# A two-layer decoder trunk: the first norm from raw rows with its vector per partition, and the group norm's turns moved to the chain's end and into the second projection

## The chip, the cores and the metric

The kernel runs on one core of a Trainium2 chip. Its time is the device time of one execution, in microseconds (us); the profile shows one execution engine by engine. TensorE (PE) multiplies matrices and transposes, VectorE (DVE), ScalarE (ACT) and GpSimd (POOL) work element by element, and transfers are issued from queues of SyncE (SP), ScalarE and POOL. TensorE's clock has two levels, 2.4 and 1.2 GHz; the profile shows what was granted, as a share of the higher.

## The reference

The input x is 256 tokens of 1024 values; there are two layers, and everything is float32. What is computed, cut down:

```python
for layer in range(2):
    h = rms_norm(x, ffn1_norm[layer])                    # x * rsqrt(mean(x*x) + eps) * g
    x = x + 0.5 * swiglu_ffn(h, ffn1_w_gu[layer], ffn1_w_down[layer])
    h = rms_norm(x, mix_norm[layer])
    p = h @ w_in                                         # gates a and b, u, v, and r, k, v, decay for the time mixing
    y_a = chunked_sgu(u_a, v_a, ...)
    y_b, v_first = rwkv7_time_mix(p_b, v_first, ...)     # a state of 64x64 per head, 16 heads, token by token
    merged = sigmoid(gate_a) * (y_a @ w_proj_a[layer]) + sigmoid(gate_b) * (y_b @ w_proj_b[layer])
    x = x + merged @ w_out[layer]
    h = rms_norm(x, ffn2_norm[layer])
    x = x + 0.5 * swiglu_ffn(h, ffn2_w_gu[layer], ffn2_w_down[layer])
return rms_norm(x, final_norm)
```

At the end of the time mixing each head of 64 values is normalised (the group norm), multiplied by gn_g, shifted by gn_b, and a bonus is added:

```python
y = (y - mu) * lax.rsqrt(var + GN_EPS)
y = y.reshape(bsz, t, B_WIDTH) * gn_g + gn_b
y = y + bonus.reshape(bsz, t, B_WIDTH)
```

## The kernel before

The 256 tokens are two blocks of 128 (tb 0 and 1). A matrix product is done in three matmuls per tile of 128 rows (`mm3`, L236 to L238): both factors are split in a high part and a low rest, and high by high, high by low and low by high are added in PSUM. "A matmul" without more means one of these, 128x512; 48 of them make a chunk: 512 columns, both blocks, 8 row tiles.

All weights come through one stream. `plan` writes down their order in units of 512 KB; `pump` issues their loads on SP's queue into three raw buffers (`wr`), and `emit_split` cuts each into `wh` (a cast on ScalarE, L220) and `wl` (a subtract on VectorE, L221), four units ahead of use. So the two engines have a weight split each 2.7 us, and whatever else they do stands between splits.

Activations are wanted with the row dimension on partitions. `transpose_split` transposes four tiles of 128x128 on TensorE (L318), casts the high part out of PSUM on ScalarE (L322), and takes the low rest on VectorE (L323).

The start: x's two blocks (512 KB each) and the first norm's vector, copied to all partitions (512 KB, L328), are loaded; VectorE multiplies x by the vector (L344), TensorE transposes, ScalarE and VectorE split, and the first chunk begins. The norm's factor per token (`rf`, L349, L350) is applied later, at the gates. `chunk_a` with token_first uses four units for block 0 and then the same four for block 1, so that block 1 may come later.

The time mixing ends in `rwkv_chain`: four steps c of 64 tokens. In each, small matmuls (64x64) make the state's input (`given` L884, L895), solve (L905), update the state (L924, with VectorE's L929 and L930), and after every second step give the output y of one token block (L942, L950). Each block's y is copied to SBUF, squared and scaled on VectorE by `rwkv_scale` (L971, L974, with a power on POOL, L973), for two groups g of four tiles. `rwkv_turn` then loads the bonus (L984), transposes (L988), multiplies and shifts with one activation per tile (L992), adds the bonus (L994) and splits (L996, L997) into `ybT`, the input of the second projection (w_proj_b). `weave` puts the chain's steps between units of other products (`gated`: gates and the first projection), so TensorE has work while a step waits for the other engines. When the chain ends, the rest of these products is done, `before()` issues the loads of the next norm on POOL's queue, and the second projection runs.

A scheduler with priorities makes each engine's order from this at build time. At run time every engine follows its own order strictly, and waits where an instruction's input isn't there.

## Time and profile before

| | |
|---|---|
| time, median of 3 runs | 1450.06 us (1449.78 to 1453.37) |
| time of the profiled execution | 1450.86 us |
| its span | 1449.2 us |
| TensorE busy | 1377.2 us (95%) |
| VectorE busy | 894.7 us (62%) |
| ScalarE busy | 735.6 us (51%) |
| mean granted clock | 0.986 |

The span is the time from the profiled execution's first to its last instruction. An engine's busy time leaves out the time in which it waits. The timeline gives for each instruction, or for a run of equal ones, its start, its length and, in brackets, how long the engine stood idle before it and what released it.

### The profile page before, as it was taken

How to read it: one execution, taken by the hardware profiler on the slowest of the kernel's cores; microseconds unless marked ns; L12 is line 12 of the kernel's file. 1: busy time of each engine (PE TensorE's matmuls, PEld its weight loads, DVE VectorE, ACT ScalarE, POOL GpSimd, SP SyncE). 2: the span in 40 equal slices, each digit the busy share in tenths (PEclk: the TensorE clock that was granted, in tenths of full speed). 3: DMA queues.
4: the chain of work that ended last, by engine and by line, in shares of the span. 5: the costliest groups of instructions: out<-in, count | busy, mean ns of one | idle time of the engine just before them, and what ended most of it. 6: DMA issues, size and time to landing. Idle time of an engine off the chain costs nothing. (4 is left out here: it accounts for less than half of the span.)

```text
span 1449.2 us, 21790 instructions
## 1 busy us (share of the span) xinstructions
PE 1377.2 (95%) x8642; PEld 1155.3 (80%) x8642; DVE 894.7 (62%) x1216; ACT 735.6 (51%) x1033; POOL 138.2 (10%) x200
## 2 busy tenths in 40 slices
PE   6999999999899999999999999999988989999996
PEld 5888879887787778888888888898867767788885
DVE  4555466769874565555555554769788636555553
ACT  5444456646555545444454443765655545545442
POOL 5000011113102110000010000110140011100000
PEclk9999999999989999999999999999999899999999
DMA  7755557443443567665576655674434425665552
GB/s 230 236 185 190 179 174 239 145 140 117 148 144 88 189 212 230 188 188 181 185 260 188 189 180 187 198 224 134 145 117 145 132 74 189 225 208 180 189 187 88
DMA packets 116871, 254.64 MB, mean 176 GB/s; under 512 B 8878, under 2 KB 12096, under 8 KB 116768
## 3 DMA queue, kind: packets, MB, share of 16 engines
q1 hardware_dynamic: 108048, 226.00, 48.7%
q0 software_dynamic: 8576, 26.72, 5.5%
q8 instruction: 68, 1.11, 0.3%
q10 hardware_dynamic: 144, 0.52, 0.1%
q14 instruction: 35, 0.29, 0.1%
HBM read 243.77 MB, written 9.44 MB: 175 GB/s over the span
## 5 line engine op out<-in xcount | busy, mean ns | idle before, releaser
L221 DVE TENSOR_TENSOR wl<-wr,wh 128x1024 fp32r<-128x1024 f32 x427 | 523.0, 1227 | 392.2 <-ACT wh L220 388.2
L220 ACT CAST wh<-wr 128x1024 fp32r<-128x1024 f32 x427 | 448.5, 1052 | 507.6 <-PE g L238 388.9
L236 PE MATMUL g<-wh,z 128*128 128x512 f32 x1088 | 431.5, 397 | 2.4 <-ACT z L322 2.4
L238 PE MATMUL g<-wh,z 128*128 128x512 f32 x1088 | 430.4, 396 | 3.3 <-DVE z L323 3.3
L237 PE MATMUL g<-wl,z 128*128 128x512 f32 x1088 | 429.2, 394 | 0.5 <-DVE wl L221 0.5
L238 PEld LDWEIGHTS g<-wh,z 128*128 128x128 f32 x1088 | 205.7, 189 | 48.5 <-DVE z L323 6.4
L236 PEld LDWEIGHTS g<-wh,z 128*128 128x128 f32 x1088 | 206.1, 189 | 45.2 <-ACT z L322 4.1
L237 PEld LDWEIGHTS g<-wl,z 128*128 128x128 f32 x1088 | 206.0, 189 | 43.2 <-DVE wl L221 1.7
L236 PE MATMUL g<-wh,w 128*128 128x512 f32 x416 | 162.9, 392 | 0.0
L237 PE MATMUL g<-wl,w 128*128 128x512 f32 x416 | 162.2, 390 | 0.0
L238 PE MATMUL g<-wh,w 128*128 128x512 f32 x384 | 149.7, 390 | 0.0
L296 PE MATMUL g<-z,wh 128*128 128x256 f32 x384 | 109.5, 285 | 0.0
L297 PE MATMUL g<-z,wl 128*128 128x256 f32 x384 | 109.3, 285 | 0.0
L294 PE MATMUL g<-z,wh 128*128 128x256 f32 x384 | 108.9, 284 | 0.0
L237 PEld LDWEIGHTS g<-wl,w 128*128 128x128 f32 x416 | 78.1, 188 | 15.8
L236 PEld LDWEIGHTS g<-wh,w 128*128 128x128 f32 x416 | 78.1, 188 | 15.7
L238 PEld LDWEIGHTS g<-wh,w 128*128 128x128 f32 x384 | 72.1, 188 | 14.9
L297 PEld LDWEIGHTS g<-z,wl 128*128 128x128 f32 x384 | 73.6, 192 | 0.5 <-issue 0.5
L296 PEld LDWEIGHTS g<-z,wh 128*128 128x128 f32 x384 | 73.7, 192 | 0.2 <-issue 0.2
L294 PEld LDWEIGHTS g<-z,wh 128*128 128x128 f32 x384 | 73.6, 192 | 0.2 <-issue 0.2
L318 PE MATMUL m<-ident,z 128*128 128x128 f32 x336 | 50.8, 277 | 17.0 <-DVE z L344 8.4
L472 POOL DMA_DIRECT2D xspill<-w x10 | 5.7, 574 | 601.7 <-DVE w L456 601.7
(232 smaller groups left out, 1256.0 us busy)
## 6 DMA issues: line engine op xcount, KB each, us to landing
wr<-in_ffn_w_gu_dram SPq DMA_DIRECT2D x176, 512.0 KB, 3.6
wr<-in_ffn_w_down_dram SPq DMA_DIRECT2D x88, 512.0 KB, 3.5
wr<-in_w_in_rest_dram SPq DMA_DIRECT2D x58, 512.0 KB, 3.5
wr<-in_w_in_first_dram SPq DMA_DIRECT2D x57, 512.0 KB, 4.0
wr<-in_w_proj_a_dram SPq DMA_DIRECT2D x16, 512.0 KB, 3.7
wr<-in_w_proj_b_dram SPq DMA_DIRECT2D x16, 512.0 KB, 3.7
wr<-in_w_out_dram SPq DMA_DIRECT2D x16, 512.0 KB, 4.0
xspill<-w POOLq DMA_DIRECT2D x10, 512.0 KB, 3.3
```

Source lines behind the costliest of these rows:

```text
L220: nc.scalar.copy(hi, raw)
L221: nc.vector.tensor_tensor(lo, raw, hi.bitcast(F32), ALU.subtract)
L236: mm(ps, lhsT=xh, rhs=wh, start=first, stop=False)
L237: mm(ps, lhsT=xh, rhs=wl, start=False, stop=False)
L238: self.last_mm = mm(ps, lhsT=xl, rhs=wh, start=False, stop=last).ins
L294: mm(o, lhsT=hi[:, k, cs], rhs=xh[kt // 4][:, kt % 4, :], start=(kt == 0 and b % 2 == 0), stop=False, skip_group_check=True)
L296: mm(o, lhsT=hi[:, k, cs], rhs=xl[kt // 4][:, kt % 4, :], start=False, stop=False, skip_group_check=True)
L297: mm(o, lhsT=lo[:, k, cs], rhs=xh[kt // 4][:, kt % 4, :], start=False, stop=kt == NK - 1, skip_group_check=True)
L318: nc.tensor.transpose(ps[:, i * P:(i + 1) * P], src[:, i * P:(i + 1) * P], self.ident)
L472: self.nc.gpsimd.dma_start(self.xsrc[tb], self.x[tb])
```

## The change

The first norm. Its vector is loaded as 8 rows of 128 values (4 KB), transposed and copied once, so that it stands per partition (`gain`). x is loaded in halves of 256 KB on SP's and ScalarE's queues, the second block behind two weight loads and two casts. TensorE transposes x itself; the vector is multiplied in when the result leaves PSUM, 128 columns at a time (ScalarE L138, VectorE L140 of the new text). The second block's turn, the squares and the factor per token of both blocks follow the first unit's six matmuls of the first chunk.

The group norm's turns. Those of token block 0, until now between the third and the fourth step of the chain (c == 2), come at the chain's end. Those of block 1, until now two steps of other work behind the chain, come into the second projection's first chunk, behind 18 matmuls (three units of block 0). In the new text the group norm's lines are L1027 (reduce), L1028 and L1029 (POOL), L1030 (scale), L1044 (transposes), L1048 (activations), L1050 (add), L1052 and L1053 (split); the chain's are L942 (`given`), L953, L963 (solve), L979 (state's input), L984 and L985 (state), L997 and L1005 (output). A weight split is L272 and L273.

```diff
+    def first_norm(self, vec, xt):
+        nc = self.nc
+        rows = self.cp.tile([NK, P], F32, name="grows")
+        nc.sync.dma_start(rows, vec.rearrange("(k p) -> k p", p=P))
+        self.x = [self.wt([P, D]) for _ in range(NTB)]
+        def load(tb):
+            r = []
+            for j, q in enumerate((nc.sync, nc.scalar)):
+                js = slice(512 * j, 512 * j + 512)
+                r.append(q.dma_start(self.x[tb][:, js], self.xsrc[tb][:, js]))
+            return r[0].ins
+        def turn(tb):
+            for j in range(2):
+                ps = self.mp().rearrange("p (k t) -> p k t", t=P)
+                for k in range(4):
+                    nc.tensor.transpose(ps[:, k, :], self.x[tb][:, (4 * j + k) * P:(4 * j + k + 1) * P], self.ident)
+                part = lambda p, k: xt[p][j][:, k, tb * P:tb * P + P]
+                g = lambda k: gain[:, 4 * j + k:4 * j + k + 1]
+                for k in range(4):
+                    hi = nc.scalar.activation(part(0, k), ps[:, k, :], AF.Identity, scale=g(k))
+                for k in range(4):
+                    lo = nc.vector.scalar_tensor_tensor(part(1, k), ps[:, k, :], g(k), part(0, k).bitcast(F32),
+                                                        ALU.mult, ALU.subtract)
+            return hi.ins, lo.ins
+        behind = self.tc.issue_after
+        first = load(0)
+        self.first_consts()
+        ps = self.mp()[:, 0:NK]
+        nc.tensor.transpose(ps, rows, self.ident[0:NK, 0:NK])
+        gain = self.cp.tile([P, NK], F32, name="gain0")
+        nc.vector.tensor_copy(gain, ps)
+        hi, lo = turn(0)
+        with behind(first), behind(hi), behind(lo):
+            self.pump(2)
+            load(1)
+        self.norm_begin()
+        def rest():
+            hi, lo = turn(1)
+            with behind(hi):
+                for tb in range(NTB):
+                    for j in range(2):
+                        self.square(tb, j)
+                    self.rf[tb] = self.norm_factor(tb, "rf")
+        return rest
 
...
-    def pump(self):
+    def pump(self, limit=1 << 30):
...
-            while self.n_load < min(len(self.units), self.n_used + RAW_BUFS + HL_BUFS - 1):
+            while self.n_load < min(limit, len(self.units), self.n_used + RAW_BUFS + HL_BUFS - 1):
...
                 us.append(self.take())
                 go(0, us[i], 2 * i)
+                if between and between[0] == i:
+                    with self.tc.issue_after(self.last_mm):
+                        between[1]()
...
+    def square(self, tb, j):
+        self.nc.scalar.activation(self.tt([P, 512]), self.x[tb][:, 512 * j:512 * j + 512], AF.Square, scale=1.0 / 32,
+                                  accum_out=self.ss[tb][:, j:j + 1])
...
-        rf = self.rf
...
-            ps = self.chunk_a(ht, ci == 0)
+            ps = self.chunk_a(ht, ci == 0, None if ci else between)
...
-                    nc.scalar.activation(t[:, tb, :g1 - c0], ps[tb][:, :g1 - c0], AF.Silu, scale=rf[tb])
+                    nc.scalar.activation(t[:, tb, :g1 - c0], ps[tb][:, :g1 - c0], AF.Silu, scale=self.rf[tb])
...
-    def load_x(self, queues):
+    def load_x(self):
         self.x = [self.wt([P, D]) for _ in range(NTB)]
         for tb in range(NTB):
-            queues[tb].dma_start(self.x[tb], self.xsrc[tb])
+            self.nc.gpsimd.dma_start(self.x[tb], self.xsrc[tb])
...
             yield
-            if c == 2:
-                for g in range(2):
-                    turn(g, 0, ys[g])
             if c < 3:
                 ps_next, last = given(c + 1)
...
-        yield
-        yield
+            if c == 1:
+                early = ys
         for g in range(2):
-            turn(g, 1, ys[g])
+            turn(g, 0, early[g])
...
-            ps = self.chunk_a(ybT, j == 0)
+            ps = self.chunk_a(ybT, j == 0, None if j else (2, self.late))
...
         with self.tc.high_priority(offset=8000):
-            before(a["ffn1_norm"][0])(True)
-            self.first_consts()
-            self.norm_begin()
-            for tb in range(NTB):
-                for j in range(2):
-                    self.norm_half(tb, j, self.g)
-                after(tb)
+            state["ht"] = self.ht()
+            rest = self.first_norm(a["ffn1_norm"][0], state["ht"])
...
-            self.ffn(l, "ffn1", state["ht"], before(a["mix_norm"][l], True), after, None if l else tables)
+            self.ffn(l, "ffn1", state["ht"], before(a["mix_norm"][l], True), after, None if l else tables,
+                     None if l else (0, rest))
```

ScalarE's order at the program's start, before. Here w is x, z the norm's result, m PSUM of transposes, wh a weight's high part:

```order
L464 DMA w_87<-in_x_dram 128x1024
L343 ACT_TABLE_LOAD
L343 ACTIVATE t_102,ss_99<-w_86 128x512
L343 ACTIVATE t_105,ss_99<-w_86 128x512
L343 ACTIVATE t_130,ss_100<-w_87 128x512
L343 ACTIVATE t_133,ss_100<-w_87 128x512
L220 CAST wh_155<-wr_153 128x1024
L220 CAST wh_161<-wr_159 128x1024
L322 CAST z_108<-m_115 128x4x128
L220 CAST wh_167<-wr_165 128x1024
L322 CAST z_109<-m_122 128x4x128
L220 CAST wh_173<-wr_171 128x1024
L322 CAST z_108<-m_139 128x4x128
L322 CAST z_109<-m_146 128x4x128
```

ScalarE's order at the same place after the change:

```order
L127 DMA w_92<-in_x_dram 128x512
L138 ACT_TABLE_LOAD
L138 ACTIVATE z_86<-m_107,gain_105 128x128 x4
L138 ACTIVATE z_87<-m_120,gain_105 128x128 x4
L272 CAST wh_135<-wr_133 128x1024
L272 CAST wh_141<-wr_139 128x1024
L127 DMA w_93<-in_x_dram 128x512
L272 CAST wh_151<-wr_149 128x1024
L138 ACTIVATE z_86<-m_179,gain_105 128x128 x4
L272 CAST wh_157<-wr_155 128x1024
L138 ACTIVATE z_87<-m_192,gain_105 128x128 x4
```

The four squares at the head are gone from here. Eight scaled copies stand ahead of the first cast instead of the squares, and the load of the second block's second half stands behind two casts.

VectorE's order in layer 0 from the first scale of block 0 (L971), before. Here gv is the scale's factor, t the output y and its square, w and ld the two halves of `ybT`:

```order
L971 TENSOR_REDUCE gv_4073<-t_4071 128x8
L974 TENSOR_TENSOR t_4068<-t_4068,gv_4073 128x512
L971 TENSOR_REDUCE gv_4083<-t_4081 128x8
L221 TENSOR_TENSOR wl_4445<-wr_4316,wh_4444 128x1024
L974 TENSOR_TENSOR t_4078<-t_4078,gv_4083 128x512
L994 TENSOR_TENSOR t_4071<-t_4071,t_4165 128x512
L997 TENSOR_TENSOR w_3714<-t_4071,w_3712 128x4x128
L929 TENSOR_TENSOR state_4220<-m_4211,state_3985 128x256
L994 TENSOR_TENSOR t_4081<-t_4081,t_4179 128x512
L930 TENSOR_TENSOR state_4220<-state_4220,ec_1821 128x256
```

VectorE's order in layer 0 from the same scale (now L1027), after:

```order
L1027 TENSOR_REDUCE gv_4097<-t_4095 128x8
L1030 TENSOR_TENSOR t_4092<-t_4092,gv_4097 128x512
L1027 TENSOR_REDUCE gv_4107<-t_4105 128x8
L1030 TENSOR_TENSOR t_4102<-t_4102,gv_4107 128x512
L273 TENSOR_TENSOR wl_4469<-wr_4312,wh_4468 128x1024
L984 TENSOR_TENSOR state_4216<-m_4207,state_4009 128x256
L985 TENSOR_TENSOR state_4216<-state_4216,ec_1845 128x256
L984 TENSOR_TENSOR state_4228<-m_4219,state_4021 128x256
L985 TENSOR_TENSOR state_4228<-state_4228,ec_1845 128x256
L1027 TENSOR_REDUCE gv_4401<-t_4399 128x8
```

The turn's add and subtract (L994, L997) are gone from here, and the four updates of the state, which were mixed with them, stand together behind both scales and a weight subtract. On TensorE 74 matmuls of other products stand between the turns of block 0, at the chain's end, and the second projection.

VectorE's order in layer 1 from the first scale of block 1, before:

```order
L971 TENSOR_REDUCE gv_10698<-t_10696 128x8
L974 TENSOR_TENSOR t_10693<-t_10693,gv_10698 128x512
L221 TENSOR_TENSOR wl_10879<-wr_10840,wh_10878 128x1024
L971 TENSOR_REDUCE gv_10708<-t_10706 128x8
L974 TENSOR_TENSOR t_10703<-t_10703,gv_10708 128x512
L221 TENSOR_TENSOR wl_10897<-wr_10858,wh_10896 128x1024
L994 TENSOR_TENSOR t_10696<-t_10696,t_10753 128x512
L997 TENSOR_TENSOR w_10007<-t_10696,w_10005 128x4x128
L994 TENSOR_TENSOR t_10706<-t_10706,t_10767 128x512
L1037 SCALAR_TENSOR_TENSOR z_10835<-z_10835,g_10921 128x512
```

VectorE's order in layer 1 from the same scale, after:

```order
L1027 TENSOR_REDUCE gv_10694<-t_10692 128x8
L1030 TENSOR_TENSOR t_10689<-t_10689,gv_10694 128x512
L273 TENSOR_TENSOR wl_10857<-wr_10813,wh_10856 128x1024
L1027 TENSOR_REDUCE gv_10704<-t_10702 128x8
L1030 TENSOR_TENSOR t_10699<-t_10699,gv_10704 128x512
L273 TENSOR_TENSOR wl_10875<-wr_10836,wh_10874 128x1024
L1050 TENSOR_TENSOR t_10388<-t_10388,t_10709 128x512
L1050 TENSOR_TENSOR t_10398<-t_10398,t_10723 128x512
L273 TENSOR_TENSOR wl_10893<-wr_10854,wh_10892 128x1024
L1053 TENSOR_TENSOR w_10031<-t_10388,w_10029 128x4x128
L1053 TENSOR_TENSOR ld_10032<-t_10398,w_10030 128x4x128
L1050 TENSOR_TENSOR t_10692<-t_10692,t_10955 128x512
```

Block 0's add and split (L1050, L1053), which stood earlier, now stand behind both scales of block 1, with weight subtracts between. On TensorE 28 matmuls of other products stand here between the turns of block 0 and the second projection.

## Rows read from the trace of the kernel before

**Rows 1.** The page, busy time of the engines over the span.

```profile
PE 1377.2 (95%) x8642; PEld 1155.3 (80%) x8642; DVE 894.7 (62%) x1216; ACT 735.6 (51%) x1033; POOL 138.2 (10%) x200
```

**Rows 2.** TensorE's waits: line, for what, us in total, times, longest us.

```profile
PE m L988 <- DVE t L974: 12.3, 7, 3.4
...
PE m L318 <- DVE z L344: 8.4, 1, 8.4
```

**Rows 3.** Timeline of TensorE at the start: start us, us, line, operation, xcount.

```profile
8.40 1.94 PE L318 MATMUL m<-ident,z 128*128 128x128 f32 x8 [8.40 <-DVE z L344]
...
11.79 0.80 PE L236 MATMUL g<-wh,z 128*128 128x512 f32 x1 [1.46 <-ACT z L322]
...
14.32 0.80 PE L238 MATMUL g<-wh,z 128*128 128x512 f32 x1 [1.03 <-DVE z L323]
...
18.75 0.52 PE L236 MATMUL g<-wh,z 128*128 128x512 f32 x1
...
27.96 0.39 PE L236 MATMUL g<-wh,z 128*128 128x512 f32 x1
```

**Rows 4.** DMA issues of the whole run: xcount, KB each, median us to landing.

```profile
bspill<-t POOLq DMA_DIRECT2D x8, 256.0 KB, 2.3
...
t<-bspill POOLq DMA_DIRECT2D x8, 256.0 KB, 3.7
...
w<-in_x_dram SPq DMA_DIRECT2D x1, 512.0 KB, 4.6
```

**Rows 5.** ScalarE's timeline in layer 0, and the page's two weight split groups.

```profile
452.56 1.50 ACT L992 ACTIVATE t<-m,vec 128x128 f32<-128x128 f32 x4 [0.16 <-PE m L988]
...
L221 DVE TENSOR_TENSOR wl<-wr,wh 128x1024 fp32r<-128x1024 f32 x427 | 523.0, 1227 | 392.2 <-ACT wh L220 388.2
...
L220 ACT CAST wh<-wr 128x1024 fp32r<-128x1024 f32 x427 | 448.5, 1052 | 507.6 <-PE g L238 388.9
```

**Rows 6.** TensorE's timeline in layer 0, end of the chain and projection.

```profile
451.90 0.63 PE L988 MATMUL m<-ident,t 128*128 128x128 f32 x4 [0.82 <-DVE t L974]
...
456.17 0.63 PE L988 MATMUL m<-ident,t 128*128 128x128 f32 x4 [2.02 <-DVE t L974]
...
456.72 1.15 PE L884 MATMUL m<-w,w 64*64 64x64 f32 x32
...
457.80 0.69 PE L924 MATMUL m<-w,bk 128*64 128x64 f32 x16
...
475.30 0.63 PE L988 MATMUL m<-ident,t 128*128 128x128 f32 x4 [1.57 <-DVE t L974]
...
479.55 0.63 PE L988 MATMUL m<-ident,t 128*128 128x128 f32 x4 [1.30 <-DVE t L974]
```

**Rows 7.** Timeline of POOL and VectorE in layer 0, same place.

```profile
451.00 1.59 POOL L984 DMA_DIRECT2D t<-bspill  x2
...
453.62 1.68 POOL L973 TENSOR_TENSOR gv<-gv,mhalf 128x8 f32<-128x8 f32 x1
...
455.32 0.69 DVE L974 TENSOR_TENSOR t<-t,gv 128x512 f32<-128x512 f32 x1 [1.85 <-POOL gv L973]
```

**Rows 8.** TensorE's timeline in layer 1.

```profile
1177.74 1.09 PE L988 MATMUL m<-ident,t 128*128 128x128 f32 x4 [3.40 <-DVE t L974]
...
1195.06 0.50 PE L236 MATMUL g<-wh,z 128*128 128x512 f32 x1
```

**Rows 9.** Busy times and granted clock (PEclk) behind that wait.

```profile
core 0: us, PE busy (x) PEld busy (x) DVE busy (x) ACT busy (x) POOL busy (x), PEclk, DMA share, GB/s
1177.74:1183.06 5.32, 5.32 (x41) 3.96 (x41) 1.59 (x2) 2.02 (x5) 0.00 (x0) 0.51 0.35 103
```

**Rows 10.** VectorE's timeline in layer 1, the second late scale.

```profile
1203.77 0.69 DVE L974 TENSOR_TENSOR t<-t,gv 128x512 f32<-128x512 f32 x1 [2.06 <-POOL gv L973]
```

**Rows 11.** TensorE's timeline in layer 1, a shorter wait elsewhere.

```profile
1089.18 0.59 PE L318 MATMUL m<-ident,z 128*128 128x128 f32 x2 [2.67 <-DVE z L540]
```

**Rows 12.** DMA issues of the first 40 us, and the second projection's over all.

```profile
wr<-in_ffn_w_gu_dram SPq DMA_DIRECT2D x13, 512.0 KB, 6.5
...
wr<-in_w_proj_b_dram SPq DMA_DIRECT2D x16, 512.0 KB, 3.7
```

More of the change, by code (lines that the diff above doesn't have):

```diff
@@ L238, in mm3, with chunk_a @@
         self.last_mm = mm(ps, lhsT=xl, rhs=wh, start=False, stop=last).ins
-    def chunk_a(self, x, token_first):
+    def chunk_a(self, x, token_first, between=None):
         xh, xl = x
@@ L342, in norm_half @@
         x = self.x[tb][:, js]
-        nc.scalar.activation(self.tt([P, 512]), x, AF.Square, scale=1.0 / 32, accum_out=self.ss[tb][:, j:j + 1])
+        self.square(tb, j)
         nc.vector.tensor_tensor(self.h[tb][:, js], x, g[:, js], ALU.mult)
@@ L368, in norm_finish, with ffn @@
             self.transpose_split(h[:, 512 * j:512 * j + 512], xt[0][j], xt[1][j], tb)
-    def ffn(self, l, n, ht, before, after, aside=None):
+    def ffn(self, l, n, ht, before, after, aside=None, between=None):
         nc, dff = self.nc, self.dff
@@ L413, in ffn @@
                         nc.vector.scalar_tensor_tensor(t[:, tb, s - lo:e - lo], ps[tb][:, s + dff - c0:e + dff - c0],
-                                                       rf[tb], gates[gc][:, tb, s - 512 * gc:e - 512 * gc],
+                                                       self.rf[tb], gates[gc][:, tb, s - 512 * gc:e - 512 * gc],
                                                        ALU.mult, ALU.mult)
@@ L957, in rwkv_chain @@
                 ys.append(scale(y))
-        yield
-        yield
+            if c == 1:
+                early = ys
         for g in range(2):
-            turn(g, 1, ys[g])
+            turn(g, 0, early[g])
+        self.late = lambda: [turn(g, 1, ys[g]) for g in range(2)]
     def rwkv_scale(self, y):
@@ L1085, in before, with f @@
         def before(vec, scaled=False):
-            def f(first=False):
+            def f():
                 state["scaled"] = scaled
-                if first:
-                    self.load_x((nc.sync, nc.scalar))
-                self.g = self.bcast(vec, self.wt, nc.sync if first else nc.gpsimd)
+                self.g = self.bcast(vec, self.wt)
                 state["ht"] = None
-                if not first:
-                    self.load_x((nc.gpsimd, nc.gpsimd))
+                self.load_x()
             return f
```

## The prediction

> **What bounds the kernel now.** I read the page first, then TensorE's list of waits, then the timeline of the three places that the change touches. TensorE is busy for 95% of the span [rows 1], so a change pays only where TensorE stands still or runs at its lower clock. The list of waits shows where: 8.4 us once, before the first transposes, and 12.3 us in seven waits of the group norm's transposes (L988) for the scale L974 [rows 2]. The change goes at both. The longest of the seven is 3.40 us in layer 1, and it costs twice: in the 5.32 us behind it the granted clock is 0.51, its lower level of 1.2 GHz, so some 2.6 us more are lost [rows 8, 9].
>
> **Part 1, the start.** Before, the transposes begin at 8.40, the first matmul at 11.79, and the third, where steady work begins, at 14.32; ten matmuls from there take 4.43 us (0.44 each, the lower level's pace), and behind the first chunk's 48 the second begins at 27.96 [rows 3]. From 18.75 on, 36 matmuls and eight transposes take 9.21 us, so a matmul at full clock costs 0.22 to 0.23.
> After the change x is transposed raw. Each block comes in two halves of 256 KB. The 512 KB load took 4.6 us to land; 256 KB took 3.7 as a load of the late values and 2.3 as a store [rows 4]. Issued at 0.8, the first block is there at 3.1 to 5.4; I take 3.7, so 4.5. Four transposes give the first bank at 5.5 (eight took 1.94 [rows 3]). Two sets of four scaled copies of 128x128 follow on ScalarE; no row has this copy with the gain alone, and the nearest, L992, takes 1.50 for four [rows 5], so both are done at 8.5. The subtracts on VectorE run beside them. The first weight cast (1.05) ends at 9.6, its subtract (1.23) at 10.8 [rows 5], and the third matmul is at 11.2 instead of 14.32.
> It doesn't stay so. After six matmuls TensorE comes to the second block's transposes at about 12.5, and that block's second half is issued by ScalarE behind two casts, at 10.6; with 2.3 to 3.7 us it lands at 12.9 to 14.3. So at 14.3 there are 42 matmuls and eight transposes left, where before 46 and eight were left. If the clock rises no earlier than before, the gain is four slow matmuls (1.7) less what transposes at the low level cost more (0.7): **1.0**. If the half lands 1.4 earlier and the clock rises 3 us earlier (seven matmuls at 0.2 less), it is 3.8, and with x itself 1.4 earlier some **4.5**. I take **2.2**, nearer to the lower end because the load of 3.7 is the nearer row. The squares and the norm factor, now behind the scaled copies, take 2.5 and a few tenths of ScalarE and VectorE and are wanted only by the first gate at the chunk's end, 10 us later: nothing.
> The Trainium skill, "ScalarE: Activation LUTs", section "What ACT_TABLE_LOAD costs", prices an ACTIVATE of N columns with one pointer operand at 280 ns + 0.833 N, less 93 ns when they follow each other. That speaks against cutting one copy into four, as the start now does, but gives 0.29 for one of 128, so an estimate of 2.4 for the eight instead of 3.0, and the sum would be up to 0.6 lower by it; [rows 5] with two operands decides here.
>
> **Part 2, layer 0.** The four waits are 0.82, 2.02, 1.57 and 1.30, together 5.7 [rows 6]. All four go, since the transposes now stand behind other work. Two new ones come.
> The first: the next chunk's state matmuls (L953 of the new text) need the state update on VectorE, and the order puts this update behind both scales and one weight subtract. The second scale started at 455.32 [rows 7]. Before it, POOL spent 1.59 on issuing two loads that are gone from there, so its power (1.68) may start up to 0.9 sooner: 454.4 to 455.3. Then come 0.69 for the scale, 1.23 for the subtract [rows 5] and 0.8 for the first group's update: 457.1 to 458.0. TensorE left L905 at 451.08 (451.90 less 0.82), and has 1.15 and twice 0.69 of small matmuls [rows 6] and three wide ones ahead, so it is there at 454.2: a wait of **2.9** to 3.8.
> The second: the late turn. In the projection's first chunk eight matmuls stand between the eight transposes and the first one that needs their result. They cover 1.8. Needed are eight activations on ScalarE (for the first group four, 1.50, but four more are ahead of the cast), add, cast and subtract, each a pass of 0.6 to 0.7 over 128x512 like [rows 10]: 1.5 + 1.5 + 0.7 + 0.6 + 0.7 less what overlaps, some 3.8. So **2.0**, between 1.0 and 2.6. The early turn has 74 matmuls (17 us) to become ready, which hide it wholly. There are also three changes fewer between small and wide matmuls; a wide one behind small ones takes about 0.2 longer with them, 0.6. Layer 0: 5.7 + 0.6 - 2.9 - 2.0 = **1.4** gained, between 0.0 and 2.6.
>
> **Part 3, layer 1.** Of the 12.3 us the other 6.6 stand here (12.3 less 5.7), and with the slow stretch 9.2 go; again 0.6 of changes. Added: the same wait for the state. The second scale freed the transposes at 1177.74 [rows 8], the update follows with 0.8 and no subtract between, and TensorE would be there at 1176.4 by the count used for layer 0: 2.1.
> Then the new bottleneck. Only 28 matmuls stand between the early turn's transposes and the projection (74 in layer 0), because less other work is left. Let T be the end of the chain's last matmul, 1195.06 before [rows 8]. TensorE comes to the projection at T + 7.0. What it needs there is the early turn's result; but VectorE's order has its adds (L1050) behind the second late scale and one more weight subtract, and the final subtracts (L1053) behind yet another. The second late scale started at 1203.77, T + 8.7 [rows 10]. So: scale to T + 9.3, subtract to T + 10.45, add to T + 11.1, cast on ScalarE to T + 11.8: first matmul. Second add and a subtract to T + 12.85, L1053 to T + 13.55: third matmul. TensorE stands 4.85 and, after two matmuls, 1.3: **6.1**. A wait of 4.85 is longer than the 3.40 behind which the clock fell, so I add 2.5 for a slow stretch like that of [rows 9]. The late turn again 2.0. Layer 1: 2.1 + 6.1 + 2.5 + 2.0 - 9.2 - 0.6 = **2.9** lost, between 0 and 5.
>
> **The sum.** 1450.86 (the profiled execution; 0.8 above the median of the three runs and inside their spread) - 2.2 - 1.4 + 2.9 = **1450.2**.
>
> **Rivals.**
> A, the forecast: the start and layer 0 give some 3.6, layer 1 takes most of it back. 1450.2; own range 1447 to 1453.5 from the ends above, not all at once.
> B, the projection of layer 1 hardly waits: the early turn's result is there before T + 9.7, within 2.67 of TensorE's arrival (a wait that left the clock up [rows 11]), and the clock stays up. For it: the early scales themselves are done 10 us before. Against it: the order of VectorE, which can't be passed. It saves 6.1 - 2.7 + 2.5 = 5.9: 1444.3.
> C, the start gives nothing: its gain up to 14.3 is lost again to the second block's half or to a clock that rises later, as its early transposes are short and followed by waits. The row of 1.0 above is near to it. 1450.2 + 2.2 = 1452.4.
> D, the clock also falls behind layer 0's wait for the state: 2.9 to 3.8 lies between a wait of 2.67 that left it up [rows 11] and the 3.40 that did not. 2.6 more: 1452.8. The Trainium skill, "TensorE: Matmul & The Clock Gate", section "HAM oscillation — how this bites in real kernels", says that waits for data drop the clock again and that the transition is paid each time; by that rule alone D would be the forecast, 1452.8. The trace agrees for the wait of 3.40, with 0.51 behind it, and not for the 2.67, behind which matmuls kept their pace.
> E, the other side: the loads of the next norm (x twice and the vector, 1.5 MB on POOL's queue) are now issued behind the late turn's loads, and so during the projections. While such loads ran at the start, weights took 6.5 us to land at the median [rows 12], where the projection's took 3.7. If this makes a unit of layer 0 late by the 2.8, and the clock falls with it (2.6), the time is 1455.6; it decides once landing eats up the lead of the units loaded ahead (seven of 2.7 us of work), which speaks against it. In layer 1 TensorE waits anyway.
>
> **How the numbers follow.** About 0.3% (4.35 us) is what a measurement of this kernel tells from no change: under 1445.7 is faster, over 1454.4 slower. Chances: A 0.50, B 0.18, C 0.12, D 0.10, E 0.10. Faster: B's 0.16 (not all of it gets below) and 0.06 of A, 0.22. Slower: E's 0.10, 0.04 of A, and 0.04 where C and D meet, 0.18. Same: 0.60. The range 1444.5 to 1455 leaves out half of B and most of E.
>
> **What would show it.** The third matmul of the start near 11.2; a wait of TensorE before the second block's transposes; 42 matmuls behind them at two paces. A wait of about 2.9 at the first L953 of the last chunk in layer 0, released by the state; none before the early turn's transposes. In layer 1 a wait of 4 to 5 at the projection's first matmul for L1052, a shorter one for L1053, and a clock of 0.5 behind it. If these last are missing, the prediction is wrong towards B; if weights release TensorE there, towards E.

## The result and the profile after

The changed kernel takes 1466.07 us (median of 4 runs, 1462.4 to 1468.8) against 1450.01 (1449.78 to 1453.37): 1.0102 times as long, 95% interval 1.0087 to 1.0118. It is slower by some 15 us, and the prediction of no change was wrong. The profiled execution took 1466.79, its span is 1465.0, the mean granted clock 0.974 for 0.986. The page's busy times after the change:

```profile
PE 1390.4 (95%) x8643; PEld 1163.8 (79%) x8643; DVE 895.1 (61%) x1225; ACT 735.6 (50%) x1045; POOL 134.3 (9%) x200
```

TensorE stood idle for 74.6 us (1465.0 less 1390.4) where it had been 72.0 [rows 1], so only 2.6 of the 15.8 us by which the span is longer are waits. The other 13.2 are the same matmuls taking longer: by the mean granted clock some 38 us of the full clock are missing in this execution (0.026 of 1465.0) and some 20 in the one before (0.014 of 1449.2). Below, a slow stretch is one in which the granted clock stands at its lower level.

Where the time went shows when one follows the wide matmuls (128x512; 4512 in both kernels, counted in order of time):

| wide matmul number | before | after | difference |
|---|---|---|---|
| 49 (second chunk) | 27.96 | 25.70 | -2.3 |
| 817 (layer 0, mixers) | 212.19 | 210.55 | -1.6 |
| 1177 (layer 0, in the chain) | 438.41 | 436.73 | -1.7 |
| 1345 (layer 0, in the second projection) | 505.61 | 514.54 | +8.9 |
| 3265 (layer 1, ahead of the chain) | 1093.61 | 1105.09 | +11.5 |
| 3745 (layer 1, behind the second projection) | 1257.93 | 1273.72 | +15.8 |

So the start gains 2.3, of which 0.6 is lost again by 210; layer 0's end of the chain and second projection lose 10.6 (from -1.7 to +8.9), layer 1's 4.3. Between the two layers another 2.6 go, in places that the change doesn't touch: 1.6 behind a wait for ScalarE in layer 1 (at the end of this document), and most of the rest at 1082 to 1086, where the clock granted is 0.57. TensorE's waits after the change (columns as in [rows 2]), the largest that are new, and one, for the norm's pass L415, that was 2.9 in total and has grown:

```profile
PE g L288 <- ACT wh L272: 6.2, 3, 3.5
PE g L288 <- ACT w L1052: 6.1, 2, 4.8
...
PE m L953 <- DVE state L985: 5.3, 2, 3.0
...
PE m L134 <- DMA w<-in_x_dram: 3.7, 2, 2.3
...
PE m L373 <- DVE z L415: 3.5, 2, 2.2
...
PE m L148 <- DMA grows<-in_ffn_norm_dram: 2.3, 1, 2.3
```

The waits of 12.3 and 8.4 in [rows 2] are gone, and somewhat more has come in their place. TensorE's timeline of the start, against [rows 3]:

```profile
4.82 1.97 PE L134 MATMUL m<-ident,w 128*128 128x128 f32 x8 [2.26 <-DMA w<-in_x_dram]
...
11.09 0.63 PE L290 MATMUL g<-wh,z 128*128 128x512 f32 x1
...
15.34 0.66 PE L134 MATMUL m<-ident,w 128*128 128x128 f32 x4 [1.49 <-DMA w<-in_x_dram]
15.75 0.47 PE L288 MATMUL g<-wh,z 128*128 128x512 f32 x1
...
25.70 0.39 PE L288 MATMUL g<-wh,z 128*128 128x512 f32 x1
```

ScalarE's scaled copies ahead of it:

```profile
5.97 2.17 ACT L138 ACTIVATE z<-m,gain 128x128 fp32r<-128x128 f32 x8 [1.84 <-PE m L134]
```

The third matmul is at 11.09 for 14.32, and the second block's late half costs 1.49. That wait is not the same in each execution. In the thirteen traces with the new start it is between nothing and 2.67, and the second chunk begins between 24.60 and 29.28 (median 26.29); in the four with the old start (the kernel before, and three of the runs below) it begins between 27.56 and 28.49. The latest of all, in e9_ahead:

```profile
16.39 0.90 PE L134 MATMUL m<-ident,w 128*128 128x128 f32 x3 [2.67 <-DMA w<-in_x_dram]
```

Layer 0, TensorE's timeline at the chain's last step and in the second projection, against [rows 6]:

```profile
455.40 0.48 PE L953 MATMUL m<-state,w 64*64 64x64 f32 x4 [3.04 <-DVE state L985]
...
491.75 0.78 PE L288 MATMUL g<-wh,w 128*128 128x512 f32 x1 [3.54 <-ACT wh L272]
493.01 0.80 PE L289 MATMUL g<-wl,w 128*128 128x512 f32 x1 [0.48 <-DVE wl L273]
...
497.52 0.79 PE L288 MATMUL g<-wh,w 128*128 128x512 f32 x1 [0.30 <-ACT wh L272]
```

And the busy times of the stretches behind these waits (columns as in [rows 9], the last three are granted clock, DMA share, GB/s):

```profile
455.00:460.00 5.00, 4.60 (x43) 2.83 (x43) 1.10 (x3) 0.65 (x2) 0.00 (x0) 0.50 0.36 105
460.00:465.00 5.00, 5.00 (x46) 3.40 (x47) 0.00 (x0) 1.27 (x4) 0.00 (x0) 0.55 0.01 3
485.00:490.00 5.00, 3.21 (x15) 2.32 (x13) 0.00 (x0) 0.00 (x0) 0.22 (x1) 1.00 1.01 339
490.00:495.00 5.00, 2.77 (x6) 1.89 (x7) 1.22 (x1) 1.54 (x2) 0.00 (x0) 0.68 1.05 286
495.00:500.00 5.00, 4.23 (x14) 2.93 (x13) 1.84 (x2) 3.58 (x9) 0.00 (x0) 0.50 0.57 160
```

Behind the wait for the state the clock is at its lower level for nearly ten us. In these the DMA engines are busy by 0.36 and 0.01; 25 us later they are full, weights are late, and the clock falls again. SP's queue shows the pause: it issued a weight load at 454.58 and the next at 474.06, where in the kernel before the next came at 463.03 (a line takes together the loads of one tensor):

```profile
463.03 34.89 SPq L206 DMA_DIRECT2D wr<-in_w_proj_b_dram  x8
```

```profile
474.06 25.06 SPq L258 DMA_DIRECT2D wr<-in_w_proj_b_dram  x7
```

And ScalarE's cast that releases TensorE at 491.75 had itself waited for a load to land:

```profile
490.65 1.04 ACT L272 CAST wh<-wr 128x1024 fp32r<-128x1024 f32 x1 [7.31 <-DMA wr<-in_w_proj_b_dram]
```

The median landing time of the second projection's weights between 470 and 500 (DMA issues of that stretch) is 8.4, and 3.7 in the same stretch of the kernel before:

```profile
wr<-in_w_proj_b_dram SPq DMA_DIRECT2D x7, 512.0 KB, 8.4
```

Layer 1, TensorE's timeline, against [rows 8]:

```profile
1190.09 0.33 PE L953 MATMUL m<-state,w 64*64 64x64 f32 x4 [2.24 <-DVE state L985]
...
1213.59 0.79 PE L288 MATMUL g<-wh,w 128*128 128x512 f32 x1 [4.82 <-ACT w L1052]
...
1215.22 0.80 PE L290 MATMUL g<-wh,w 128*128 128x512 f32 x1 [0.41 <-DVE w L1053]
...
1224.42 0.50 PE L288 MATMUL g<-wh,w 128*128 128x512 f32 x1 [1.32 <-ACT w L1052]
```

The first two waits are for the early turn's result, the third is for the late turn's.

The busy times behind layer 1's wait for the state, where the clock granted is 0.65 on average for ten us:

```profile
1190.00:1195.00 5.00, 4.91 (x55) 3.04 (x57) 1.93 (x4) 0.65 (x2) 0.00 (x0) 0.65 0.31 104
1195.00:1200.00 5.00, 5.00 (x81) 3.83 (x79) 0.00 (x0) 1.27 (x4) 0.00 (x0) 0.66 0.01 4
```

### The profile page after: what moved, and what is told of

The parts are those of the page before. It is cut to its first block, busy times and chain, and to the rows that moved or that the text cites. A ratio compares the mean times of both kernels' runs of the same rounds, so it can differ in the third digit from the quotient of the medians.

```text
span 1465.0 us, 21802 instructions
## 1 busy us (share of the span) xinstructions
PE 1390.4 (95%) x8643; PEld 1163.8 (79%) x8643; DVE 895.1 (61%) x1225; ACT 735.6 (50%) x1045; POOL 134.3 (9%) x200
## 5 line engine op out<-in xcount | busy, mean ns | idle before, releaser
L273 DVE TENSOR_TENSOR wl<-wr,wh 128x1024 fp32r<-128x1024 f32 x427 | 522.8, 1227 | 392.6 <-ACT wh L272 388.6
L272 ACT CAST wh<-wr 128x1024 fp32r<-128x1024 f32 x427 | 448.7, 1053 | 512.1 <-PE g L290 370.6
L288 PE MATMUL g<-wh,w 128*128 128x512 f32 x416 | 165.5, 398 | 10.0 <-ACT w L1052 6.1
L290 PE MATMUL g<-wh,w 128*128 128x512 f32 x384 | 150.8, 393 | 0.4 <-DVE w L1053 0.4
L373 PE MATMUL m<-ident,z 128*128 128x128 f32 x320 | 47.8, 274 | 9.6 <-DVE z L598 5.5
```

Source lines behind the costliest of these rows:

```text
L272: nc.scalar.copy(hi, raw)
L273: nc.vector.tensor_tensor(lo, raw, hi.bitcast(F32), ALU.subtract)
L288: mm(ps, lhsT=xh, rhs=wh, start=first, stop=False)
L290: self.last_mm = mm(ps, lhsT=xl, rhs=wh, start=False, stop=last).ins
L373: nc.tensor.transpose(ps[:, i * P:(i + 1) * P], src[:, i * P:(i + 1) * P], self.ident)
```

## The experiments

Ratios are to the kernel before, run on the same chip beside each kernel, with the 95% interval. Slow stretches are read from windows of 2 us over the whole span.

**The two parts alone, and the two turns alone.** e1_start keeps part 1 and has chain and turns as before; e2_turns is the reverse. e3_early and e4_late have the new start and one moved turn each (edits against the changed kernel):

```diff
 # e3_early: block 0's turn at the chain's end, block 1's as before
         for g in range(2):
             turn(g, 0, early[g])
-        self.late = lambda: [turn(g, 1, ys[g]) for g in range(2)]
+        yield
+        yield
+        for g in range(2):
+            turn(g, 1, ys[g])
...
-            ps = self.chunk_a(ybT, j == 0, None if j else (2, self.late))
+            ps = self.chunk_a(ybT, j == 0)
 # e4_late: block 0's turn at c == 2 as before, block 1's in the projection
+            if c == 2:
+                for g in range(2):
+                    turn(g, 0, ys[g])
...
-            if c == 1:
-                early = ys
-        for g in range(2):
-            turn(g, 0, early[g])
```

> The start's part alone; chain and turns as before. Both theories: the trace after the change shows the second chunk beginning 2.3 us sooner (25.70 for 27.96), so 1447.7, between 1446.5 and 1449.5. If it came out at 1450 or above, the gain of the start is given back later.

> The turns' part alone; the start as before. If the two parts add up: the changed kernel's 1466.1 plus the 2.3 of the start, 1468.4, between 1464 and 1471. If the parts disturb each other through loads or the clock, it lies outside.

> New start; block 0's turn at the chain's end as in the change, block 1's turn two steps behind the chain as before, none in the projection. Theory I (the early turn's move costs: the state waits behind the scales on VectorE, few wide matmuls are left in the chain and the clock falls behind it): a wait for the state of 2 to 3 in each layer, clock 0.5 behind it for 7 to 9 us, and about 1454 (1447.7 plus 4 in layer 0 and 2 in layer 1). Theory II (only the late turn's place costs, with weights that land late behind the next norm's loads): about 1447.7.

> New start; block 0's turn between the third and the fourth step as before, block 1's turn in the second projection as in the change. Theory I: hardly slower than the start alone, 1449 (two waits of some 1.5 in the projections less two of as much behind the chain). Theory II: in layer 0 weights land late behind the loads of the next norm, waits of 3.5 and more for a weight cast and a slow stretch: about 1456 (1447.7 plus 5 of waits and 3 of clock).

Measured: e1_start 1451.0 (1.0007, 0.9997 to 1.0018), e2_turns 1466.56 (1.0107, 1.0089 to 1.0124), e3_early 1460.43 (1.0069, 1.0054 to 1.0085), e4_late 1452.73 (1.0012, 1.0001 to 1.0023). So the turns cost all of it, and of these the early one alone about 9 (e3_early less e1_start); the late one alone 1.7, which is within the noise. Together they cost some 4 more than the two add up to. Theory I has the place right and the price too low by 6 (1454 for e3_early). Theory II's late weights don't appear in e4_late's trace: TensorE waits for no weight in layer 0's projection there. The start gives nothing, though its second chunk begins 3.3 sooner in its trace: a question of its own, below.

**The state first.** On VectorE the state's update stands behind both scales and a weight subtract after the change. VectorE's timeline of the changed kernel:

```profile
452.72 0.69 DVE L1030 TENSOR_TENSOR t<-t,gv 128x512 f32<-128x512 f32 x1 [2.05 <-POOL gv L1029]
453.33 1.22 DVE L273 TENSOR_TENSOR wl<-wr,wh 128x1024 fp32r<-128x1024 f32 x1
454.47 0.42 DVE L984 TENSOR_TENSOR state<-m,state 128x256 f32<-128x256 f32 x1
```

e5_state issues the scales of block 0 behind the update:

```diff
-                    TTm(new, new, ec, ALU.mult)
+                    state = TTm(new, new, ec, ALU.mult).ins
...
                 S[c + 1][g] = new
+            if c == 2:
+                with self.tc.issue_after(state):
+                    early = [scale(y) for y in early]
...
-                ys.append(scale(y))
+                ys.append(scale(y) if c == 3 else y)
```

> The changed kernel, with block 0's scales issued behind the third state update, so that VectorE updates the state first. Theory I (the wait of 3.0 and 2.2 for the state is what drops the clock behind it): both waits shrink below 1, no slow stretch behind them, 5.1 of clock deficit less in layer 0 and 3.4 in layer 1; about 1456 (1466 less 2.3 and 1.5 of waits less some 6 of slow work). Theory II (the clock falls since hardly any wide matmuls are left in this stretch, wait or not): waits shrink, the slow stretch stays, about 1462.

Measured: 1450.08 (0.9994, 0.9982 to 1.0006), 16 us less than the changed kernel. VectorE's timeline of this kernel:

```profile
447.86 0.42 DVE L984 TENSOR_TENSOR state<-m,state 128x256 f32<-128x256 f32 x1 [6.83 <-PE m L979]
...
449.45 1.27 DVE L1030 TENSOR_REDUCE gv<-t 128x8 f32<-128x512 f32 x2
```

The update now starts right behind TensorE's product, at 447.86, and the other passes follow. The busy times of the stretches behind it:

```profile
450.00:455.00 5.00, 5.00 (x75) 3.47 (x73) 1.68 (x4) 2.25 (x5) 4.22 (x4) 1.00 0.02 3
455.00:460.00 5.00, 5.00 (x136) 4.33 (x135) 1.56 (x2) 1.72 (x7) 0.00 (x0) 1.00 0.36 108
```

No wait for the state is left in TensorE's list, and the clock stays up. So the order on VectorE, with the state behind the scales, is what costs, and theory II's forecast, a slow stretch that stays, fails. Whether the clock fell by the wait alone is not separated: the edit also leaves 14 wide matmuls between the third step's solve and the chain's last matmul, where the changed kernel has 10. More came back than theory I's 10 (1456 was forecast): layer 1's wait for the early turn shrinks too (4.82 to 2.5), and the slow stretches at 1038 and 1082 are not in this trace, which nothing in the edit explains. A wait of 2.74 for a weight cast in layer 0 remains, with a slow stretch behind it.

**The loads.** e6_loads, e7_both and e8_mid move `before()`, which issues the next norm's loads, behind the second projection in the text; e7_both and e8_mid also have the state first, and e8_mid has block 1's turn two steps behind the chain.

```diff
-        before()
 ...
+        before()
         ps = [self.chunk_a(mT, True) for _ in range(2)]
```

> The changed kernel, with the next norm's loads (x twice and the vector, 1.5 MB) issued behind the second projection instead of at its start. Theory III (these loads delay the weights of the projection in layer 0): the wait of 3.54 for a weight cast and its three followers are gone, and so is the slow stretch behind them, about 1458 (1466 less 4.8 less 3). Theory IV (the weight splits come late since ScalarE's casts stand behind the turn's cast): the wait stays, about 1466.

> The edits of the two kernels before this one together. If theories I and III hold and add up: about 1448; if II and III: 1454; if I and IV: 1456; if II and IV: 1462.

> New start; block 0's turn at the chain's end with its scales behind the state update; block 1's turn two steps behind the chain as in the kernel before; next norm's loads behind the second projection. No turn inside the projection. If I and III hold, the waits behind the chain stay (some 3 in each layer) and the wait of 3.4 with its slow stretch in layer 1 is gone: about 1446. If II holds: 1453.

Measured: e6_loads 1464.82 (1.0103), e7_both 1449.28 (0.9999, 0.9989 to 1.0008), e8_mid 1444.83 (0.996, 0.9945 to 0.9975). The edit did nothing: nothing holds these loads, and POOL issued them at 481.59 where it had been 480.97. e6_loads tells nothing of theory III, and e7_both only repeats e5_state. e8_mid, the state first and no turn in the projection, is a version that beats the kernel before. The next three are the changed kernel (e9_ahead), e5_state (e10_state_ahead) and e8_mid (e11_mid_ahead) with the loads issued from inside the chain, ahead of the early turn, so that POOL has them ahead of the group norm's powers:

```diff
+        loads()
         for g in range(2):
             turn(g, 0, early[g])
...
-        before()
```

> The changed kernel, with the next norm's loads put ahead of the group norm's powers on POOL's queue, so that they go out while the chain still runs and the DMA engines are idle (the edit tried before left them at their place: they were issued at 482 as in the changed kernel). Theory III (these loads delay the weights of layer 0's projection): weights land in some 4 instead of 8.4, the wait of 3.5 for a weight cast and the slow stretch behind it are gone, about 1458. Theory IV (the weight casts are held up behind the turn's cast on ScalarE and so the next loads): the wait stays, about 1465.

> The state update first (as in the run that gave 1450.1), and the next norm's loads ahead as in the kernel before this one. III: the wait of 2.7 and its followers in layer 0 go with their slow stretch of 5.1, about 1443.5. IV: about 1450.

> The version with block 1's turn behind the chain (1444.8), with the loads ahead too. III: two waits of 0.8 for weights in layer 0 less and a slow stretch of 1.7, about 1442. IV: 1444.8.

Measured: e9_ahead 1462.19 (1.0078, 1.0063 to 1.0093), e10_state_ahead 1448.47 (0.9982, 0.9973 to 0.9992), e11_mid_ahead 1441.39 (0.9935, 0.992 to 0.995). The landing of layer 0's second projection's weights in e9_ahead (DMA issues):

```profile
wr<-in_w_proj_b_dram SPq DMA_DIRECT2D x7, 512.0 KB, 6.8
```

And TensorE's first wait for them there:

```profile
491.93 0.49 PE L288 MATMUL g<-wh,w 128*128 128x512 f32 x1 [2.19 <-ACT wh L272]
```

Landing 6.8 for 8.4, the wait 2.19 for 3.54, the time 3.9 less (intervals 1.0063 to 1.0093 and 1.0087 to 1.0118, so at the edge of the noise): theory III is right for a part. The rest of the lateness stays, and in e10_state_ahead the wait is 2.60, hardly less than e5_state's 2.74. In e11_mid_ahead, with no turn inside the projection, no wait for weights is left in layer 0, where e8_mid had two of 0.8; the landing there:

```profile
wr<-in_w_proj_b_dram SPq DMA_DIRECT2D x7, 512.0 KB, 4.6
```

**What else makes the weights late.** e13_cast is e10_state_ahead with the turn's high part copied on VectorE, since ScalarE's weight casts stood behind it:

```diff
-        nc.scalar.copy(hi, z)
+        nc.vector.tensor_copy(hi, z)
```

> The kernel with the state first and the loads ahead, late turn in the projection (1448.5), with the turn's high part copied on VectorE instead of ScalarE, so that ScalarE's weight casts don't stand behind it. Theory IV (the casts are held up 2.9 to 3.4 us behind that copy, so raw buffers come free late and weights are loaded late): the wait of 2.6 for a weight cast in layer 0 is gone, about 1445. Otherwise (the projection's first chunk takes four units in half the usual time, and no order of the casts helps): the wait stays, about 1448.5.

Measured: 1449.53 (0.9991, 0.9981 to 1.0001). TensorE's wait in layer 0:

```profile
483.61 0.49 PE L288 MATMUL g<-wh,w 128*128 128x512 f32 x1 [0.50 <-ACT wh L272]
```

The wait fell from 2.60 to 0.50, so theory IV is right for this wait; the time didn't follow. Slow stretches came at 210, 264, 1070, 1206 and 1192 to 1200 that e10_state_ahead has not, or shorter. The trace can't tell the edit's worth from them.

**Where the start's gain goes.** s1_shift and s2_shift are the kernel before with block 0 multiplied by the norm vector two and four times, which delays all that follows; e12_old_start is e11_mid_ahead with the old start.

```diff
-        nc.vector.tensor_tensor(self.h[tb][:, js], x, g[:, js], ALU.mult)
+        for _ in range(1 + getattr(self, 'extra', 0)):
+            nc.vector.tensor_tensor(self.h[tb][:, js], x, g[:, js], ALU.mult)
...
 # s1_shift; s2_shift has 3 * (1 - tb)
+                self.extra = 1 - tb
```

> The kernel before, with the multiplication of block 0 by the norm vector done twice at the start (1.3 us more of VectorE, same result), so that all that follows is shifted and nothing else is changed. Theory S (the waits of 1.5 to 2.7 that are in all these kernels drop the clock or not by when they fall, and the kernel before falls well): slower by more than the shift, 1453 to 1456, with slow stretches at other places and a spread of several us. Theory R (the start's gain is given back by something that its own edits cause): 1451.4, the shift alone, and the same slow stretches as before.

> The kernel before, block 0 multiplied by the norm vector four times instead of once. With twice, 1.1 us of it were hidden (the first matmul stood at 11.84 for 11.79); with four times the first matmul comes some 2 us later. Theory S: the shift moves where the slow stretches fall, so the time differs from 1452.3 (before plus 2) by a couple of us either way, with a spread of 3 or more and other stretches in the trace. Theory R: 1452.3 with the stretches of the kernel before.

> The fastest version so far (1441.4: block 0's turn at the chain's end with the state updated first, block 1's turn two steps behind the chain, loads ahead) with the start of the kernel before, so without the change's first part. Orders from the chain on are the same. Theory S (the start's 3 us are real, and are hidden in other comparisons by where slow stretches fall): 1444.5. Theory R (the start gives nothing in the end): 1441.5.

Measured: s1_shift 1451.31 (1.0003, 0.9993 to 1.0012), s2_shift 1453.05 (1.0016, 1.0006 to 1.0026), e12_old_start 1439.54 (0.9926, 0.9912 to 0.9941). In s1_shift the delay was hidden (first matmul 11.84 for 11.79), so it says little. In s2_shift the second chunk began 1.6 later and the kernel took 2.3 more: about what a delay carried through to the end would cost. Slow stretches do move (to 264, 370, 1074, 1090) and the spread is 4.3, as theory S said, but the median is theory R's 1452.3 within a us; the run doesn't decide between the two. And yet the old start is not slower in the fastest version: e12_old_start is 1.9 below e11_mid_ahead, within the noise. Part of the answer stands above: the new start's own gain varies with the landing of x's late half. The timelines of the two kernels that differ in the start alone show another part in layer 0's first mixer norm, on VectorE, POOL and TensorE. The kernel before:

```profile
209.48 1.26 DVE L356 TENSOR_SCALAR z<-z,rs 128x512 f32<-128x512 f32 x1 [0.68 <-POOL rs L350]
209.51 2.12 POOL L582 MEMSET w<- 64x1024 f32 x2
210.88 1.07 PE L318 MATMUL m<-ident,z 128*128 128x128 f32 x8 [1.61 <-DVE z L356]
```

And e1_start:

```profile
207.45 2.15 DVE L415 TENSOR_SCALAR z<-z,rs 128x512 f32<-128x512 f32 x1 [0.69 <-POOL rs L409]
...
207.47 1.85 POOL L640 MEMSET w<- 64x1024 f32 x2
209.75 1.06 PE L373 MATMUL m<-ident,z 128*128 128x128 f32 x8 [2.39 <-DVE z L415]
```

Where no write of POOL stands beside it, such a pass takes 0.48, as this one of the kernel before:

```profile
200.14 0.48 DVE L356 TENSOR_SCALAR z<-z,rs 128x512 f32<-128x512 f32 x1
```

In the traces before the next edit it took 1.26 in each of the five with the old start and 2.15 in each of the twelve with the new. TensorE waits some 0.8 longer, and right behind it the clock falls in seven of the twelve and in none of the five. e14_new_start_memset and e15_old_start_memset write the zeros on VectorE:

```diff
-            nc.gpsimd.memset(lo[64:128, :, :].bitcast(F32), 0.0)
+            nc.vector.memset(lo[64:128, :, :].bitcast(F32), 0.0)
```

> The version with the new start, early turn at the chain's end, state first and loads ahead (1441.4), with the zeros of the decay weights' lower half written by VectorE instead of POOL. In every trace with the new start the norm's scaling pass on VectorE behind the first feed-forward takes 2.15 us beside two such writes of POOL, with the old start 1.26, alone 0.48; TensorE waits 2.2 to 2.5 for 1.5 there, and in most of these traces the clock falls behind it. Theory P (there the start's gain goes): the pass takes 0.5, the wait is about 0.9, no slow stretch at 210, about 1438.5. If the pass is long for another reason: 1441.5.

> The same edit on the version with the old start (1439.5). Theory P: the pass takes 0.5 for 1.26, about 1438.7; then the new start is worth up to 2.7 more with this edit than without: the kernel before this one should be as fast or faster than this one, where without the edit it was 1.9 slower. If not, the start's gain goes elsewhere as well.

Measured: e14_new_start_memset 1438.45 (0.9906, 0.9891 to 0.992), e15_old_start_memset 1439.81 (0.9919, 0.9904 to 0.9935). In e14's trace:

```profile
207.86 0.49 DVE L415 TENSOR_SCALAR z<-z,rs 128x512 f32<-128x512 f32 x1 [0.68 <-POOL rs L409]
...
208.50 0.63 PE L373 MATMUL m<-ident,z 128*128 128x128 f32 x4 [0.62 <-DVE z L415]
```

The pass takes 0.49, TensorE waits 0.62, no slow stretch follows at 210, and the new start's time is 2.9 less by the edit (intervals 0.992 to 0.995 and 0.9891 to 0.992), while the old start's doesn't change within its spread. In e15_old_start_memset the pass takes 0.48, so there it had cost less to begin with:

```profile
210.85 0.63 PE L318 MATMUL m<-ident,z 128*128 128x128 f32 x4 [1.03 <-DVE z L356]
```

With the edit the new start is 1.4 ahead, where it was 1.9 behind. That POOL's writes make the pass long and TensorE wait is shown. That this is the whole of the lost gain is not, nor that the new start is worth its 3 us: the intervals of e14 and e15 overlap, as those of e11 and e12 do, and e14's trace has a slow stretch that e11's has not:

```profile
260.00:264.00 4.00, 3.33 (x16) 3.33 (x17) 1.28 (x3) 2.49 (x7) 0.59 (x1) 0.61 0.41 167
```

e14 has the lowest time of all versions, some 13 us below the kernel before.

## Why the prediction was wrong

The step that failed is Part 2's sum for layer 0, 1.4 gained, where 10.6 were lost. It left the clock up behind the wait for the state, put nothing for late weights, and so counted waits alone. The slow stretch behind the state's wait is missing from layer 1's sum too.

- **The start.** The third matmul was forecast at 11.2 and stood at 11.09, the gain at the second chunk at 2.2 and was 2.3 in this trace. Both are in part luck. The eight scaled copies took 2.17 for the 3.0 of the sum, while x came 0.3 later. The second block's late half came at 15.3 where 12.9 to 14.3 was forecast, and against that full pace came 3.0 sooner than before (15.75 for 18.75), which only the upper end of the forecast had. Of the 2.3, 1.7 were still there ahead of the loss in layer 0's chain, so in this kernel the start isn't what failed. But the sum carries its gain to the end, and e1_start shows none of it there: 0.9 goes in a pass of VectorE that stands beside POOL's zeros, more in the clock behind it in some executions, and the rest stays open.
- **Layer 0's wait for the state.** Forecast 2.9, measured 3.04. What failed is the choice that no slow stretch follows it, made by one row, the wait of 2.67 that had none [rows 11]. The clock fell behind 3.04 here and behind 2.24 in layer 1. Rival D had the mechanism, with 2.6; the clock granted in 455 to 465 was 0.50 and 0.55, so some 4.8 of these ten us were lost, and it came in both layers.
- **Layer 0's weights.** Rival E had the place and, with 2.8 and 2.6, about half the price: waits of 3.54, 0.48, 0.30 and 0.47 and a slow stretch from 492 to 502. I set against it that seven units are loaded ahead. But between the third step's solve and the chain's last matmul stand 10 wide matmuls for 24, so few units are used, no buffer comes free, and SP issues no load for 19.5 us. Then units are wanted in one burst. That POOL's loads share the engines and that ScalarE's casts stand behind the turn's cast each make a part of the lateness (e9_ahead, e13_cast); how large the burst's own part is, no run shows.
- **D and E as separate rivals.** They were given 0.10 each, as if one excluded the other. They came together, and e5_state, which takes away D's wait and leaves 2.74 of E's, shows that they have causes of their own.
- **Layer 1.** The forecasts of 4.85 for the early turn's result and 2.1 for the state were met by 4.82 and 2.24, and that for the third matmul (1.3) by 0.41. The loss was 4.3 for 2.9, the slow stretch behind the state's wait being what was missing.
- **The late turn.** Forecast 2.0 in each layer; measured 1.32 in layer 1 and nothing in layer 0, where the slow matmuls ahead of it took long enough. The prediction counts eight matmuls that cover it; in the trace of layer 1 there are six. e4_late, which has this turn alone, is 1.7 above the start alone. The size was no error that mattered.

What is not settled: why the clock falls behind one wait and not behind another of the same length, and how much of the 1.7 between e1_start and e4_late is such a stretch.

## What to carry to other kernels

When work moves, look first at what it now stands in front of on the engine that serves the critical chain: here two passes of the group norm, put ahead of a small update of the state, cost some 16 us, as much as the whole change lost. Price a wait of TensorE together with the slow stretch that may follow it, and count what is left of wide matmuls in a chain of small ones, because they also pace the weight stream: here the next load came 19.5 us after the last. A gain at the start may be gone at the next collision downstream, so look there before it is put into a sum.

## What the runs showed of the hardware

The norm's pass of VectorE (TENSOR_SCALAR, 128x512, from SBUF to SBUF) took 0.48 us alone and 1.26 or 2.15 beside two POOL writes of zeros of 64x1024. The two writes together took 1.85 where the pass took 2.15, and 2.12 where it took 1.26. So the pass stood behind both writes (1.67 above its 0.48) or behind one (0.78 above it), and in the second case the other write gave way by 0.27. This looks like a turn taken whole, and not like a rate that is shared. The Trainium skill says as much (SBUF — State Buffer, section Who interferes with whom): a `tensor_scalar` of VectorE that uses both ports and an instruction of GpSimd exclude each other for their whole length. The traces agree. By their start times VectorE's pass came first in all of them, by 0.02 to 0.04 us, and yet stood behind at least one write. Behind how many went with the start and was the same in every trace of one kind; what decides it the runs don't show.

The same wait may or may not drop the clock. In layer 1 both kernels wait alike for ScalarE. TensorE's timeline of the kernel before, and the windows behind it:

```profile
1027.13 0.39 PE L689 MATMUL m<-w,w 96*128 96x256 f32 x1 [1.58 <-ACT w L665]
```

```profile
1027.00:1033.00 6.00, 5.87 (x34) 5.03 (x35) 3.79 (x6) 4.90 (x12) 0.00 (x0) 1.00 0.38 118
```

And the same two of the changed kernel:

```profile
1036.22 0.39 PE L747 MATMUL m<-w,w 96*128 96x256 f32 x1 [1.57 <-ACT w L723]
```

```profile
1036.00:1042.00 6.00, 5.78 (x25) 4.92 (x26) 3.10 (x5) 4.28 (x11) 0.00 (x0) 0.72 0.39 117
```

The waits differ by 0.01, and the clock is granted in full behind the one and at 0.72 on average behind the other. This alone is 1.6 of the 15.8 us between the two traces, and no part of the change stands there.
